# A hybrid diffusion step on one core: attention preparation moved beside the neighbourhood attention, and a changed opening

## The chip, the cores and the metric

One core of one Trainium2 chip runs the whole program in one launch. TensorE is called PE here, VectorE DVE, ScalarE ACT, GpSimd POOL, SyncE SP. The metric is the device time of one execution in microseconds (us); the profile's span is the part of it that the hardware profiler covers.

## The reference: what is computed

Two identical mixer layers (DEPTH = 2, width 2048) over 384 tokens: 128 context tokens and 256 latent tokens. Each layer normalises and modulates x (adaLN), projects it once to 7184 columns, runs four head groups on slices of the projection, gates each, and projects the concatenation back:

```
mod = silu(cond) @ ada_w + ada_b;  shift, scale, gate = split(mod, 3)
xm = rmsnorm(x, norm_w) * (1 + scale) + shift
pr = split_projection(xm @ w_in)
out_a = (rglru(conv(lru_x), forward) + rglru(..., backward)) * silu(lru_gate)
out_b = natten_latent(na_q, na_k, na_v, cache, rpb) * silu(na_gate)      # 4 heads
gq = rmsnorm(gqa_q, qnorm); gk = rmsnorm(gqa_k, knorm)                   # per head
out_c = attention(axial_rope(gq), [axial_rope(gk), cache]) * silu(gqa_gate)
out_d = rmsnorm(mlstm both directions) * sigmoid(ml_o) * silu(ml_gate)
x = x + gate * (concat(out_a, out_b, out_c, out_d) @ w_out)
```

Context tokens use a second conditioning vector and read only context. The caches of keys, values and recurrent states are outputs too. All is fp32.

## The kernel before, in words

PE multiplies fp32 by three rounded products: a weight tile arrives by DMA as `raw`, ACT copies it to a rounded `wh` (L193), POOL subtracts to get the rest `wl` (L1284), and PE adds xh·wh, xl·wh and xh·wl (L1402) into one of four accumulator banks (`acc`) or one of two scratch banks (`s`). The same is done to x: `xh` on ACT, `xl` on DVE (L469).

The modulation matrix is too large to sit on PE's path, so it is streamed as `araw` and summed on DVE, one 128x512 multiply-add at a time, into the PSUM tile `sbp` (L197, the first of a piece at L334). A finished piece is folded by two transposes and two reduces (L347, L348), a small matmul (L302) and a few tiny DVE operations (L305, L308, L312). The first two k-tiles are an exception: PE makes their modulation (`ada_pe`), from which `modulate0` builds the first `xh` and `xl`.

The opening follows a written list, START: "P" steps are pieces of that first modulation, "x" loads, "w" weights, "D" the first DVE modulation pieces, and "r" the multiplication of the x tiles `xr` by the reciprocal root mean square (`unit_rms`, L458): six tiles on DVE in one go, ten tiles later on POOL, in two pieces each, issued from `modulate0` four tiles ahead.

After it, one plan holds weight visits and modulation pieces in order. With each visit the planner's clock moves by PE's estimated time (`tick`), and whenever it has passed a due time the current branch generator is advanced one step: mLSTM, then LRU (`br_lru`), then neighbourhood attention (`br_na`, four heads, each a front of scores on the two `s` banks and a back), then grouped-query attention (`br_gqa`). A step's yield, multiplied by PACE, says how much PE time shall pass to the next. A scheduler then orders each engine's instructions by these positions, and every engine runs its list strictly in that order. Deferred jobs (`defer`) run at a given time of the same clock: `setup_params` (L230), twenty tiny DVE operations that make constants for the LRU and the mLSTM, at 60 us after the start of layer 0's modulation.

`br_gqa` begins with its preparation: 18 ACT squares of 128x128 with an accumulator read each, a square root with a Newton step (L401, L402), 18 DVE multiply-multiplies by root and norm weight, 16 DVE operations of rotary positions (L1034, L1038, L1039). Then come transposes, scores, softmax and the products.

Weights, layer constants and caches travel on SP's queue in issue order; some outputs on ACT's.

## Time and profile before

| what | value |
|---|---|
| three runs | 1468.54, 1468.83, 1475.76 us; median 1468.83 |
| profiled execution | 1480.24 us, span 1478.4 us |
| mean granted PE clock over the span | 0.975 of full |
| PE / DVE / ACT / POOL busy | 96% / 73% / 56% / 62% |

A row of a timeline gives start and duration in us, engine, line, operation, what it writes and reads, and in brackets how long the engine stood idle before it and which engine and tile released it. "xN" means N instructions run together. Lines are those of the kernel before. A granted clock of 1.00 is 2.4 GHz; the other level that the rows show is half of it.

### The profile page before, as it was taken

The page shows a single profiled execution, that of the slowest core. Times are in us where ns is not written, and L with a number is a line of the kernel's source. Part 1 is how long each engine was busy: PE and PEld are TensorE (multiplying, and loading weights), DVE is VectorE, ACT ScalarE, POOL GpSimd, SP SyncE. Part 2 cuts the span into 40 slices and gives each one's busy share as a digit, 9 for nine tenths or more (in the row PEclk, how much of TensorE's full clock was granted, in tenths as well). Part 3 has the DMA queues.
Part 4 walks back from the last instruction along what each step waited for, and adds up shares of the span by engine and source line. Part 5 has one row for each costly group of instructions (what it writes and reads, how often), then busy time and mean ns, then how long its engine had stood idle before and what let it go on. Part 6 is the DMA issues. An engine that isn't in the chain of part 4 may idle for free. (4 is left out here: it accounts for less than half of the span.)

```text
span 1478.4 us, 23865 instructions
## 1 busy us (share of the span) xinstructions
PE 1415.2 (96%) x7999; PEld 1331.2 (90%) x7999; DVE 1080.4 (73%) x2050; ACT 828.1 (56%) x1638; POOL 914.5 (62%) x1242
## 2 busy tenths in 40 slices
PE   6889999899999999999989999999999999899997
PEld 1879999798998799999989999999999789799997
DVE  4889999998899948858568998447667760943533
ACT  4579999765546776553343434234454877363432
POOL 1856666656566765755737666675656774555762
PEclk7899999999999999999999999999999999899999
DMA  8777878686677555565748877654547344355433
GB/s 271 242 231 250 240 230 253 197 253 180 180 209 239 163 165 161 206 222 195 233 130 263 249 243 231 181 159 122 173 142 232 100 128 133 104 175 171 146 122 96
DMA packets 167519, 281.67 MB, mean 191 GB/s; under 512 B 17380, under 2 KB 49380, under 8 KB 167268
## 3 DMA queue, kind: packets, MB, share of 16 engines
q1 hardware_dynamic: 159520, 272.40, 60.4%
...
q8 instruction: 62, 1.02, 0.3%
...
## 5 line engine op out<-in xcount | busy, mean ns | idle before, releaser
L1284 POOL TENSOR_TENSOR wl<-raw,wh 128x256 fp32r<-128x256 f32 (+1 forms) x1152 | 864.9, 785 | 477.5 <-ACT wh L193 414.3
L1402 PE MATMUL acc<-xh,wh 128*128 128x384 f32 x1630 | 568.1, 349 | 20.0 <-ACT xh L193 10.0
L1402 PE MATMUL acc<-xl,wh 128*128 128x384 f32 x1630 | 554.2, 340 | 0.0
L1402 PE MATMUL acc<-xh,wl 128*128 128x384 f32 x1630 | 552.2, 339 | 0.2 <-POOL wl L1284 0.2
L197 DVE SCALAR_TENSOR_TENSOR sbp<-araw,pers,sbp 128x512 f32<-128x512 f32 x690 | 517.6, 750 | 27.2 <-DMA araw<-in_ada_n 15.6
L193 ACT ACTIVATE wh<-raw 128x1024 fp32r<-128x1024 f32 (+2 forms) x304 | 307.0, 1013 | 324.9 <-PE acc L1402 248.6
L1402 PEld LDWEIGHTS acc<-xh,wh 128*128 128x128 f32 x1630 | 309.0, 190 | 25.7 <-ACT xh L193 10.4
L1402 PEld LDWEIGHTS acc<-xl,wh 128*128 128x128 f32 x1630 | 308.6, 189 | 1.5
L1402 PEld LDWEIGHTS acc<-xh,wl 128*128 128x128 f32 x1630 | 308.1, 189 | 1.2 <-POOL wl L1284 1.1
L1402 PE MATMUL acc<-wh,xl 128*128 128x512 f32 (+2 forms) x452 | 165.4, 366 | 5.4 <-DVE xl L469 2.7
L1402 PE MATMUL acc<-wl,xh 128*128 128x512 f32 (+2 forms) x452 | 163.9, 363 | 0.0
L1402 PE MATMUL acc<-wh,xh 128*128 128x512 f32 (+2 forms) x452 | 163.0, 361 | 0.0
L1402 PEld LDWEIGHTS acc<-wh,xl 128*128 128x128 f32 x452 | 88.5, 196 | 19.3 <-DVE xl L469 4.6
L1402 PEld LDWEIGHTS acc<-wl,xh 128*128 128x128 f32 x452 | 88.0, 195 | 12.5
L1402 PEld LDWEIGHTS acc<-wh,xh 128*128 128x128 f32 x452 | 88.0, 195 | 12.1
L197 DVE SCALAR_TENSOR_TENSOR cat<-acc,pers,xold 128x128 f32<-128x128 f32 (+1 forms) x56 | 20.3, 409 | 66.7 <-PE acc L1402 66.7
L193 ACT ACTIVATE cat<-acc 128x384 f32<-128x384 f32 (+1 forms) x94 | 46.2, 495 | 5.4 <-PE acc L1402 4.8
L193 ACT ACT_TABLE_LOAD x26 | 33.4, 1283 | 10.2 <-DVE arena L891 7.9
L193 ACT ACTIVATE xh<-cat 128x384 fp32r<-128x384 f32 x32 | 16.5, 519 | 40.0 <-PE acc L1402 24.0
L389 DVE TENSOR_TENSOR arena<-arena,sq 128x384 f32<-128x384 f32 x38 | 25.8, 679 | 16.0 <-ACT sq L193 14.5
L1402 PE MATMUL s<-xh,wh 128*128 128x384 f32 x98 | 34.1, 348 | 1.2 <-ACT cat L193 1.2
L334 DVE TENSOR_SCALAR sbp<-araw,pers 128x512 f32<-128x512 f32 x46 | 34.3, 745 | 0.2
(338 smaller groups left out, 1824.0 us busy)
## 6 DMA issues: line engine op xcount, KB each, us to landing
...
```

What stands on the lines that cost most here:

```text
L193: return nc.scalar.activation(out, in_, f, bias=bias, scale=scale)
L197: return nc.vector.scalar_tensor_tensor(out, a, s, b, op0=op0, op1=op1)
L334: d = nc.vector.tensor_scalar(acc, raw, sc, None, op0=OP.mult)
L389: eng.tensor_tensor(sqacc, sqacc, s, op=OP.add)
L1284: nc.gpsimd.tensor_tensor(it["lo"][:, kk, cs], raw[:, kk, cs], hv[:, kk, cs], op=OP.subtract)
L1402: last_ev["pe"] = nc.tensor.matmul(out, a, b, start=s0 and i == 0, stop=s1 and i == 2, skip_group_check=not it["first"]).ins
```

## The change

A new generator `gqa_prep` takes the GQA preparation out of `br_gqa` and stands in a side queue of its own (`prepq`), which `tick` advances by its own clock whenever no `br_lru` is among the branch generators; what is left of it is run when `br_gqa` begins. Its steps are smaller. Sums of squares are 9 ACT squares of 128x256 and 9 DVE reduces; the normalisation is 18 ACT copies with a scale and 9 DVE products of 128x256; the rotary part has 24 DVE operations. Its constants `gqk` are loaded at its start, behind the last layer load.

In the opening, `ada_pe` ends with three DVE operations on precomputed `nb0`, DVE normalises four x tiles in step "r" and POOL the other twelve, `setup_params` is deferred to 228 and its DVE operations are ordered behind the last modulation multiply-add issued, PACE is 1.12, and two yields of `br_lru` are longer.

```diff
--- before.py
+++ after.py
@@ -103,8 +103,8 @@
     PRE = {0: True, 1: False}
     KG = {0: [2, 2, 2, 2, 2, 2, 2, 2], 1: [8, 8]}
     START = "PxPPxPPxPPxrPDDwwDD"
-    PACE = 1.1
-    clock = dict(now=0.0, due=0.0)
+    PACE = 1.12
+    clock = dict(now=0.0, due=0.0, side=0.0)
     deferred = []
     backlog = []
 
...
@@ -235,6 +235,11 @@
         nc.vector.tensor_scalar(hbi, P("bi"), 0.5, None, op0=OP.mult)
         nc.vector.tensor_scalar(mln, P("mlnorm"), 0.25, None, op0=OP.mult)
 
+    def late_setup():
+        for ins in traced(setup_params):
+            if ins.engine == mybir.EngineType.DVE:
+                order(ins, last_ev["ada"])
+
 
     ada_acc = dict(done=0)
     last_ev = {}
@@ -256,14 +261,8 @@
                 last_ev["v"] = ins
 
 
-    def ada_final_mod(l, j0, nj):
-        v = mod[:, l, j0:j0 + nj, :]
-        b = P("ada_b", l)[:, j0:j0 + nj]
-        nc.vector.tensor_tensor(v, v, b[:, :, None].to_broadcast([128, nj, 2]), op=OP.add)
-        if 16 <= j0 < 32:
-            nb = P("norm", l)[:, j0 - 16:j0 - 16 + nj]
-            stt(Amul[:, l, j0 - 16:j0 - 16 + nj, :], v, 1.0, nb[:, :, None].to_broadcast([128, nj, 2]),
-                OP.add, OP.mult)
+    nb0 = pers(2)
+    stt(nb0, P("ada_b", 0)[:, 16:18], 1.0, P("norm", 0)[:, 0:2], OP.add, OP.mult)
 
     sbp = pada.tile([128, 1024], F32, name="sbp")
 
@@ -282,9 +281,14 @@
             pt = scr("adat")
             for q in range(4):
                 nc.tensor.transpose(pt[:, 2 * q:2 * q + 2], row[0:2, q * 128:(q + 1) * 128], ident[0:2, 0:2])
-            for i, j0 in enumerate((0, 16)):
-                nc.vector.tensor_copy(mod[:, 0, j0:j0 + 2, :], pt[:, 4 * i:4 * i + 4].rearrange("p (q c) -> p q c", c=2))
-                ada_final_mod(0, j0, 2)
+            pv = pt[:, 0:8].rearrange("p (q c) -> p q c", c=2)
+
+            def per_k(v):
+                return v[:, 0:2][:, :, None].to_broadcast([128, 2, 2])
+
+            nc.vector.tensor_tensor(mod[:, 0, 0:2, :], pv[:, 0:2], per_k(P("ada_b", 0)), op=OP.add)
+            nc.vector.tensor_tensor(Amul[:, 0, 0:2, :], pv[:, 2:4], per_k(P("norm", 0)), op=OP.mult)
+            nc.vector.tensor_tensor(Amul[:, 0, 0:2, :], Amul[:, 0, 0:2, :], per_k(nb0), op=OP.add)
             ada_acc["done"] += 1
 
     quarter = pers(4)
@@ -334,6 +338,7 @@
                 d = nc.vector.tensor_scalar(acc, raw, sc, None, op0=OP.mult)
             else:
                 d = stt(acc, raw, sc, acc, OP.mult, OP.add)
+            last_ev["ada"] = d.ins
             if "v" in last_ev:
                 order(d.ins, last_ev["v"])
 
@@ -467,8 +472,8 @@
                                     op0=OP.mult, op1=OP.add)
         xl[k] = big.tile([128, T], F32R, name=f"xl{k}", tag=f"xl{k}", bufs=1)
         nc.vector.tensor_sub(xl[k], t, xh[k].bitcast(F32))
-        if 6 <= k + 4 < KC:
-            unit_rms(k + 4, nc.gpsimd)
+        if 4 <= k + 2 < KC:
+            unit_rms(k + 2, nc.gpsimd)
 
     def split_cat(k):
         act(xh[k], cat[:, k, :], AF.Copy)
@@ -640,7 +645,7 @@
         lay_seq += [(I["mlk"], 512, "mlk", 1)] + [(I["mlc"][l, h], 258, "mlc", 2) for h in range(4)]
         lay_seq += [(I["lw"][l, g], 512, "lw", 2) for g in range(4)]
         lay_seq += [(I["nac"][l, h, :, 0:576], 576, "nac", 2) for h in range(4)]
-        lay_seq += [(I["gqk"][l], 768, "gqk", 1)] + [(I["gqc"][l, h], 256, "gqc", 2) for h in range(2)]
+        lay_seq += [(I["gqc"][l, h], 256, "gqc", 2) for h in range(2)]
     lay_next = []
     last_dma = {}
 
@@ -870,7 +875,7 @@
                 act(uu[d], aa[d], AF.Tanh, bias=nls4[:, cs], scale=nls4[:, cs])
                 act(aa[d], aa[d], AF.Exp, bias=ls4[:, cs], scale=ls4[:, cs])
                 stt(ww[d], ww[d], 1.0, xc, OP.add, OP.mult)
-                yield 3.0
+                yield 3.0 + 0.5 * d
             if g < 3:
                 xn = conv(g + 1)
             tq = wrk.tile([128, NJ], F32, name="tq", tag="t15", bufs=4)
@@ -898,7 +903,7 @@
             else:
                 nc.vector.tensor_add(cat[:, g, :], hh[0], hh[1])
             mark(g)
-            yield 4.0
+            yield 5.0
         defer(6.0, lambda: nc.scalar.dma_start(O["lru"][l], lout))
 
 
@@ -993,58 +998,71 @@
         yield from attention(front, prep)
 
 
+    def gqa_prep(l):
+        gq, kk = S["gqa_q"], S["gqa_k"]
+        gqk = lay.tile([128, 784], F32, name="gqk", tag="gqk", bufs=1)[:, 0:768]
+        order(nc.sync.dma_start(gqk, I["gqk"][l]).ins, last_dma["d"])
+        nc.scalar.dma_start(O["gqa_v"][l], S["gqa_v"][:, 0, :])
+        ss = slot("gss")
+
+        def pairs(t):
+            for c in range(3):
+                ap = kk[:, t, :] if c == 2 else gq[:, t, c * 256:c * 256 + 256]
+                yield ap, t * 6 + 2 * c, gqk[:, 640:768] if c == 2 else gqk[:, 512:640]
+
+        def tmp(name):
+            return wrk.tile([128, T], F32, name=name, tag="t15", bufs=4)[:, 0:256]
+
+        for t in range(3):
+            for ap, i, _ in pairs(t):
+                sq = tmp("gsq")
+                act(sq, ap, AF.Square)
+                nc.vector.tensor_reduce(ss[:, i:i + 2], sq.rearrange("p (h n) -> p h n", h=2), axis=AX.X, op=OP.add)
+            yield 2.5
+        root = sm(10, 18, "groot")
+        act(root, ss, AF.Sqrt, bias=epsc, scale=1.0 / 128)
+        nc.vector.tensor_scalar(ss, ss, 1.0 / 128, EPS, op0=OP.mult, op1=OP.add)
+        rms_newton(root, ss, sm(11, 18, "gnewt"))
+        rq = root.rearrange("p (t h) -> p t h", t=3)[:, :, 0:4]
+        nc.vector.tensor_scalar(rq, rq, SC, None, op0=OP.mult)
+        yield 3.0
+        for t in range(3):
+            for ap, i, wn in pairs(t):
+                for h in range(2):
+                    hs = slice(h * 128, h * 128 + 128)
+                    act(ap[:, hs], ap[:, hs], AF.Copy, scale=root[:, i + h:i + h + 1])
+                x3 = ap.rearrange("p (h n) -> p h n", h=2)
+                nc.vector.tensor_tensor(x3, x3, wn[:, None, :].to_broadcast([128, 2, 128]), op=OP.mult)
+            yield 3.0
+        for t in range(2):
+            cos = gqk[:, t * 128:(t + 1) * 128]
+            s4 = gqk[:, 256 + t * 128:256 + (t + 1) * 128].rearrange("p (a s f) -> p a s f", a=2, s=2)
+            for ap, _, _ in pairs(1 + t):
+                rot = tmp("rot")
+                r5 = rot.rearrange("p (h a s f) -> p h a s f", h=2, a=2, s=2)
+                x5 = ap.rearrange("p (h a s f) -> p h a s f", h=2, a=2, s=2)
+                for s in range(2):
+                    nc.vector.tensor_tensor(r5[:, :, :, s, :], x5[:, :, :, 1 - s, :],
+                                            s4[:, :, s, :][:, None, :, :].to_broadcast([128, 2, 2, 32]),
+                                            op=OP.mult)
+                x3 = ap.rearrange("p (h n) -> p h n", h=2)
+                nc.vector.tensor_tensor(x3, x3, cos[:, None, :].to_broadcast([128, 2, 128]), op=OP.mult)
+                nc.vector.tensor_add(ap, ap, rot)
+                yield 1.5
+        nc.scalar.dma_start(O["gqa_k"][l], kk[:, 0, :])
+
     def br_gqa(l):
+        while prepq:
+            advance_side()
         gq = S["gqa_q"]
         kk = S["gqa_k"]
         gv = S["gqa_v"]
-        gqk = next_lay()
-        qn, kn = gqk[:, 512:640], gqk[:, 640:768]
-        nc.scalar.dma_start(O["gqa_v"][l], gv[:, 0, :])
-        ss = slot("gss")
-        junk = slot("ktm")
-
...
-        for t in range(2):
-            cos = gqk[:, t * 128:(t + 1) * 128]
-            sin = gqk[:, 256 + t * 128:256 + (t + 1) * 128]
-            for ap, nh, wi in ((gq[:, 1 + t, :], 4, 0), (kk[:, 1 + t, :], 2, 1)):
-                rot = w(wi, "rot")[:, 0:nh * 128]
-                r5 = rot.rearrange("p (h a s f) -> p h a s f", h=nh, a=2, s=2)
-                x5 = ap.rearrange("p (h a s f) -> p h a s f", h=nh, a=2, s=2)
-                s4 = sin.rearrange("p (a s f) -> p a s f", a=2, s=2)
-                for s in range(2):
-                    nc.vector.tensor_tensor(r5[:, :, :, s, :], x5[:, :, :, 1 - s, :],
-                                            s4[:, :, s, :][:, None, :, :].to_broadcast([128, nh, 2, 32]),
-                                            op=OP.mult)
-                x3 = ap.rearrange("p (h n) -> p h n", h=nh)
-                nc.vector.tensor_tensor(x3, x3, cos[:, None, :].to_broadcast([128, nh, 128]), op=OP.mult)
-                nc.vector.tensor_add(ap, ap, rot)
-            yield 4.0
-        nc.scalar.dma_start(O["gqa_k"][l], kk[:, 0, :])
         qT = cm(six("gqT"))
         kT = cm(six("gkT"))
         for h in range(6):
             p_ = scr("gt")
             for t in range(3):
-                ap = heads(t)[h][0]
+                ap = gq[:, t, h * 128:(h + 1) * 128] if h < 4 else kk[:, t, (h - 4) * 128:(h - 3) * 128]
                 nc.tensor.transpose(p_[:, t * 128:(t + 1) * 128], ap, ident)
             act(qT[:, h, :] if h < 4 else kT[:, h - 4, :], p_[:, :T], AF.Copy)
             if h == 5:
@@ -1076,9 +1094,20 @@
 
 
     fillers = []
+    prepq = []
 
     def start(fn):
-        return lambda l: fillers.append(fn(l))
+        def f(l):
+            fillers.append(fn(l))
+            if fn is br_gqa:
+                prepq.append(gqa_prep(l))
+        return f
+
+    def advance_side():
+        try:
+            clock["side"] = max(clock["side"], clock["now"] - 4.0) + PACE * next(prepq[0])
+        except StopIteration:
+            prepq.pop(0)
 
     gk_get = lazy("gqa_k", lambda t: t, lambda key: wts.tile([128, 3, 256], F32, name="gqa_k", tag="gqa_k", bufs=1))
 
@@ -1346,6 +1375,8 @@
             need(*mods[0][1:])
         while fillers and clock["due"] <= clock["now"]:
             advance()
+        while prepq and clock["side"] <= clock["now"] and all(g.__name__ != "br_lru" for g in fillers):
+            advance_side()
 
     accs = {}
     turn = [0, 0]
@@ -1556,7 +1587,7 @@
             upto("w", wl, w_dma, pos["w"] + 1)
         elif tok == "r":
             rstd_bc()
-            for k in range(6):
+            for k in range(4):
                 unit_rms(k, nc.vector)
         elif tok == "P":
             it = first.pop(0)
@@ -1589,7 +1620,7 @@
                 for k in it["ks"]:
                     need(l, k)
                 if l == 0:
-                    defer(60.0, setup_params)
+                    defer(228.0, late_setup)
         elif ty == "split":
             whole.clear()
             for n4 in range(2):
```

DVE in layer 1, kernel before: the end of the fourth neighbourhood-attention head (L986), then the preparation, in which `arena`, `cat` and `gqa_k` are its tiles, and the first gate operation `gth`.

```order
L986 ISA arena,nm<-s_79,nabias 128x384
L986 ISA nm 128x1
L916 RECIPROCAL rs<-ssum 128x3
L1015 TENSOR_SCALAR arena<-arena 128x18
...
L197 SCALAR_TENSOR_TENSOR cat<-cat,arena,gqk 128x128 x4
L197 SCALAR_TENSOR_TENSOR gqa_k<-gqa_k,arena,gqk 128x128 x2
L1034 TENSOR_TENSOR arena<-cat,gqk 128x8x32
...
L1038 TENSOR_TENSOR cat<-cat,gqk 128x512
L197 SCALAR_TENSOR_TENSOR gth<-gth,acc_112 128x384
```

Nothing of the preparation stands among the heads, and the gate waits for its place in the list behind it.

DVE in layer 1, changed kernel: from the second head's scores (L991) over preparation operations to the third head's.

```order
L991 ISA arena,nm<-s_79,nabias 128x384
L991 ISA nm 128x1
L1020 TENSOR_REDUCE arena<-gsq 128x2 x3
...
L1035 TENSOR_TENSOR cat<-cat,gqk 128x256 x2
L1035 TENSOR_TENSOR gqa_k<-gqa_k,gqk 128x256
L1035 TENSOR_TENSOR cat<-cat,gqk 128x256
L1045 TENSOR_TENSOR rot<-cat,gqk 128x4x32 x2
...
L1050 TENSOR_TENSOR cat<-cat,rot 128x256
L988 TENSOR_REDUCE nm<-s_79 128x1
L991 ISA arena,nm<-s_79,nabias 128x384
```

All 42 operations of the preparation now stand between the heads of the neighbourhood attention, and the first gate operation follows the fourth head with no preparation in front:

```order
L1050 TENSOR_TENSOR gqa_k<-gqa_k,rot 128x256
L988 TENSOR_REDUCE nm<-s_80 128x1
L991 ISA arena,nm<-s_80,nabias 128x384
L991 ISA nm 128x1
L991 ISA arena,nm<-s_79,nabias 128x384
L991 ISA nm 128x1
L921 RECIPROCAL rs<-ssum 128x3
L197 SCALAR_TENSOR_TENSOR gth<-gth,acc_113 128x384
```

In these rows `nm` and `s` belong to a head's scores; the gate moved from behind the preparation to behind the head.

DVE in the opening, kernel before: the last two of six x tiles, then the end of `ada_pe` (`pers` holds the modulation), up to the first modulated tile `xmt`.

```order
L458 TENSOR_TENSOR xr_94<-xr_94,pers 128x384
L458 TENSOR_TENSOR xr_95<-xr_95,pers 128x384
L286 COPY pers<-s_80 128x4 x2
L262 TENSOR_TENSOR pers<-pers 128x4
L197 SCALAR_TENSOR_TENSOR sbp<-araw,pers,sbp 128x512
L262 TENSOR_TENSOR pers<-pers 128x4
L197 SCALAR_TENSOR_TENSOR sbp<-araw,pers,sbp 128x512
L197 SCALAR_TENSOR_TENSOR pers<-pers 128x4
L197 SCALAR_TENSOR_TENSOR sbp<-araw,pers,sbp 128x512
L466 TENSOR_SCALAR xmt<-xr_90,pers 128x128
```

The first modulated tile stands behind eight operations here. The same place in the changed kernel, which goes on to the pick that ends the first modulation piece (L309, L305 before):

```order
L463 TENSOR_TENSOR xr_93<-xr_93,pers 128x384
L289 TENSOR_TENSOR pers<-s_80,pers 128x4
L290 TENSOR_TENSOR pers<-s_80,pers 128x4
L291 TENSOR_TENSOR pers<-pers 128x4
L197 SCALAR_TENSOR_TENSOR sbp<-araw,pers,sbp 128x512
L471 TENSOR_SCALAR xmt<-xr_90,pers 128x128
...
L197 SCALAR_TENSOR_TENSOR sbp<-araw,pers,sbp 128x512 x27
...
L338 TENSOR_SCALAR sbp<-araw,pers 128x512 x2
L197 SCALAR_TENSOR_TENSOR sbp<-araw,pers,sbp 128x512 x4
L309 TENSOR_TENSOR picked<-s_80,pers 128x32
```

Three small operations and one `sbp` stand where five and three stood, and the set-up operations, which before were interleaved with `sbp` from here on, are gone. They now stand in layer 0's first mLSTM head (`ls` and `pers` of 128x16):

```order
L717 SCALAR_TENSOR_TENSOR arena<-s_80,pers 128x256
L212 RECIPROCAL ls_3567<-ls_3567 128x16
L721 TENSOR_TENSOR arena<-arena,mlk 128x384
L213 TENSOR_TENSOR ls_3566<-ls_3566,ls_3567 128x16
L721 TENSOR_TENSOR arena<-arena,mlk 128x384
```

L717 and L721 are the scan and product of that head; the set-up stands between them.

## Rows read from the trace of the kernel before

**Rows 1.** Page: busy time of each engine, share of span, instructions.

```profile
PE 1415.2 (96%) x7999; PEld 1331.2 (90%) x7999; DVE 1080.4 (73%) x2050; ACT 828.1 (56%) x1638; POOL 914.5 (62%) x1242
```

**Rows 2.** Timeline, PE: instructions that began after a wait, and one pick.

```profile
39.38 0.69 PE L1402 MATMUL acc<-xh,wh 128*128 128x384 f32 x1 [5.77 <-ACT xh L193]
...
77.58 0.30 PE L302 MATMUL s<-red,pers 128*128 128x32 f32 x2
...
85.61 0.69 PE L1402 MATMUL acc<-xh,wh 128*128 128x384 f32 x1 [4.27 <-ACT xh L193]
...
351.95 0.49 PE L796 MATMUL s<-ml_v,arena 128*128 128x129 f32 x2 [2.28 <-DVE arena L197]
...
496.19 0.69 PE L865 MATMUL s<-xcs,lwh 128*128 128x388 f32 x2 [3.39 <-DVE picked L305]
...
1176.65 1.02 PE L865 MATMUL s<-xcs,lwh 128*128 128x388 f32 x2 [3.13 <-ACT arena L193]
...
1275.78 0.69 PE L1402 MATMUL acc<-xh,wh 128*128 128x384 f32 x1 [6.99 <-DVE gth L197]
```

**Rows 3.** Stretches: us; PE, PEld, DVE, ACT, POOL busy; PE clock; DMA share; GB/s.

```profile
39.38:49.38 10.00, 8.45 (x38) 7.62 (x39) 10.00 (x21) 6.15 (x11) 10.00 (x18) 0.67 0.67 194
85.61:95.61 10.00, 9.35 (x46) 8.54 (x47) 6.18 (x12) 5.75 (x14) 1.26 (x2) 0.76 0.65 231
95.00:260.00 165.00, 165.00 (x963) 159.66 (x962) 153.62 (x259) 156.20 (x323) 108.29 (x151) 1.00 0.79 238
282.48:292.48 10.00, 8.73 (x38) 7.91 (x39) 9.04 (x16) 6.40 (x13) 7.62 (x12) 0.70 0.64 190
351.95:361.95 10.00, 10.00 (x50) 9.88 (x51) 10.00 (x20) 5.19 (x15) 6.59 (x9) 0.83 0.98 298
496.19:506.19 10.00, 10.00 (x39) 8.32 (x40) 9.96 (x19) 7.43 (x12) 6.26 (x8) 0.83 0.44 130
525.00:600.00 75.00, 75.00 (x441) 73.34 (x439) 52.53 (x118) 46.75 (x115) 45.79 (x52) 1.00 0.54 157
1176.65:1186.65 10.00, 10.00 (x33) 8.36 (x34) 2.75 (x5) 8.90 (x16) 5.16 (x7) 0.70 0.46 135
1206.00:1257.00 51.00, 51.00 (x283) 47.07 (x282) 11.41 (x34) 35.89 (x97) 25.69 (x37) 1.00 0.47 135
1275.78:1285.78 10.00, 10.00 (x42) 10.00 (x43) 10.00 (x20) 1.89 (x3) 1.29 (x2) 0.71 0.10 38
```

**Rows 4.** Timeline, DVE, layer 1's preparation.

```profile
1261.30 2.58 DVE L197 SCALAR_TENSOR_TENSOR cat<-cat,arena,gqk 128x128 f32<-128x128 f32 x4
...
1267.37 0.95 DVE L1034 TENSOR_TENSOR arena<-cat,gqk 128x256 f32<-128x256 f32 x1
...
1268.98 0.41 DVE L1034 TENSOR_TENSOR arena<-cat,gqk 128x256 f32<-128x256 f32 x1
...
1275.18 0.54 DVE L197 SCALAR_TENSOR_TENSOR gth<-gth,acc 128x384 f32<-128x384 f32 x1
```

**Rows 5.** Opening: DVE and ACT timeline, and POOL's groups by form (31 to 95).

```profile
31.31 4.43 DVE L458 TENSOR_TENSOR xr<-xr,pers 128x384 f32<-128x384 f32 x6 [0.57 <-ACT pers L193]
...
38.34 1.86 ACT L193 ACTIVATE xh<-xr,pers 128x128 fp32r<-128x128 f32 x4 [1.17 <-DVE pers L197]
...
L458 POOL TENSOR_TENSOR xr<-xr,pers 128x256 f32<-128x256 f32 x10 | 7.4, 737 | 0.0
```

**Rows 6.** Timeline, DVE, end of the first modulation piece.

```profile
76.34 5.51 DVE L197 SCALAR_TENSOR_TENSOR sbp<-araw,pers,sbp 128x512 f32<-128x512 f32 x7
81.75 0.18 DVE L305 TENSOR_TENSOR picked<-s,pers 128x32 f32<-128x32 f32 x1
```

**Rows 7.** Groups of DVE by line, 44 to 68: the set-up's multiply-adds.

```profile
L197 DVE SCALAR_TENSOR_TENSOR ls<-ls,ls 128x16 f32<-128x16 f32 x7 | 3.0, 424 | 0.0
```

**Rows 8.** Timeline, ACT: before the mLSTM wait, and the LRU's table load.

```profile
347.70 1.06 ACT L193 ACTIVATE wh<-raw 128x1024 fp32r<-128x1024 f32 x1 [3.96 <-DMA raw<-in_w_in]
...
1174.72 1.28 ACT L193 ACT_TABLE_LOAD   x1 [2.72 <-DVE arena L891]
```

20 lines of the change are left out of this document (1 added, 19 removed).

## The prediction

> **What bounds the kernel now.** I read the page's busy line first, then the PE instructions that stood idle before they began, then a table of stretches for the clock behind each of those stalls, and last the DVE and ACT lines in front of each stall. The busy line [rows 1] is to show that PE is the bound: busy 1415.2 us of a span of 1478.4, so all its idle time is 1478.4 − 1415.2 = 63.2 us, and nothing that the change does to DVE, ACT or POOL counts unless it lengthens or shortens one of PE's waits. [rows 2] has the six longest waits that the edits can reach: 5.77 us at 39.38 (the first projection matmul), 4.27 at 85.61, 2.28 at 351.95 (mLSTM, layer 0), 3.39 at 496.19 (LRU, layer 0), 3.13 at 1176.65 (LRU, layer 1), 6.99 at 1275.78. They sum to 25.8 us. Behind each, [rows 3] shows PE's granted clock below 1.00 in the ten microseconds that begin with the restart: the lower of the two levels, 1.2 GHz, in place of 2.4. While the clock is halved PE does half as much, so ten microseconds at a mean clock c lose (1 − c)·10: 3.3 (first matmul), 2.4 (85.61), 3.0 (282.48), 1.7 (351.95), 1.7 (496.19), 3.0 (1176.65), 2.9 (1275.78). In stretches in which PE did not stand (95 to 260, 525 to 600, 1206 to 1257) the same column reads 1.00. A removed stall of some us therefore gives back its own length and two or three us more.
>
> **Part by part. K, layer 1's GQA preparation (1257 to 1276).** Up to the fourth neighbourhood-attention (NA) head DVE is nearly free: 11.41 us busy of the 51 from 1206 to 1257 [rows 3]. Then the normalise and rotary operations come in a block, from 128x128 operations at 2.58/4 = 0.65 us each (1261.30) through rotary products, and the gate operation `gth` that frees PE's accumulator bank stands behind them until 1275.18; PE restarts 0.6 us later [rows 2, 4]. In the new order the whole preparation stands ahead of that gate, between the four NA heads' operations. Gone are the 6.99 us and the 2.9 us of low clock: −9.9.
>
> What the moved preparation costs: 9 reduces, 9 norm products and 24 rotary operations on DVE, 42 in all, none longer in elements than 128x256. At 0.41 us (the quicker 128x256 row, 1268.98) they take 42·0.41 = 17.2 us, at 0.95 (the same operation at 1267.37) 42·0.95 = 39.9. DVE's room is 51 − 11.4 = 39.6 us in layer 1 and 75 − 52.5 = 22.5 in layer 0 [rows 3], where part of the old preparation already lies in that stretch. I take the quick end, since POOL works only half of either stretch (25.69 of 51, 45.79 of 75), and book +2 (0 to +5) for NA heads whose scores wait on DVE behind the preparation, in layer 1.
> The same row pair is the place for a rule. 1267.37 and 1268.98 are one operation, with two SBUF inputs, at 0.95 and 0.41 us [rows 4]. The Trainium skill ("SBUF — State Buffer", section "Who interferes with whom") says that a VectorE instruction with two SBUF inputs contends with a GpSimd instruction that reads SBUF, and that whichever starts second is blocked until the other is done. The 0.54 us between the two rows fit that. By the rule every one of the moved products can meet POOL's weight subtraction; what it would do is the slower rival below.
>
> ACT gets 18 scaled copies of 128x128. The nearest row is `xh` at 1.86/4 = 0.47 us each [rows 5]: 8.4 us, and 9 squares of 128x256, between one and two of those each, 4.2 to 8.4. It loses the 18 squares. Two activation-table loads are added as the root falls among the NA exponentials: 1.28 us each by the row at 1174.72 [rows 8]. ACT is free 15.1 us of 51 in layer 1 and 28.2 of 75 in layer 0 [rows 3], so this hides, but not in layer 0 between the last two NA heads: there six norm products and eighteen copies stand in front of the gate evacuations of one PE group. Before, that place cost nothing (PE is busy 75.00 of 75). I book +1.5 (0 to +4). The preparation's own DMA goes on SP's queue behind the last layer load and no longer ahead of the GQA caches; two ACT-queue stores come earlier. Neither has a waiter on PE before the attention: 0.
>
> **A, the opening.** DVE normalises six xr tiles in 4.43 us, 0.74 each, from 31.31, then runs seven small or modulation-weight operations, and ACT's `xh` starts at 38.34 [rows 5]. Four tiles end at 31.31 + 2.95 = 34.26 and three 128x4 operations replace the seven: `xh` can start near 36.5. Gain 1.8 of the 5.77. The low clock behind it stays, since 4 us of idle remain. POOL inherits two tiles, 4 operations at up to 0.74 (its 128x256 mean there) = 3.0 us ahead of weight subtractions that PE needs next; if they land on PE they eat the gain and 1.2 us more, and if low clock goes as well the gain is at most 3. −1.8 (−3 to +2); SP's weight DMAs wait for these subtractions too, and the modulation weights queue behind them.
>
> **B, the stall at 85.61.** PE delivered the sum at 77.58, yet DVE's pick stands behind seven `sbp` operations (5.51 us) until 81.75, a lateness of 4.2 us [rows 2, 6]. DVE was late by the parameter set-up: seven 128x16 operations take 3.0 us, 0.42 each [rows 7]; the other thirteen are no larger, and at half of that or all of it they add 2.8 to 5.5: I take 3, so 6 in all. All twenty leave this stretch, and four `sbp`, not seven, stand before the pick. That covers 4.2 us, so the stall falls to about zero or one, and with it most of the low clock's 2.4: −5.5 (−6.7 to 0; 0 if the modulation-weight transfers, not DVE, set the pace).
> **D, 278 to 292.** The modulation chain ends here; DVE is busy 153.62 of 165 us before it [rows 3]. PE arrives up to 7 us earlier and DVE loses only the set-up and its idle: a small wait may grow. +1 (−2 to +3, the low end if its low clock goes).
> **E, the set-up at its new place.** The twenty operations, 6 us, now stand among mLSTM head 0's DVE chain, ahead of its scores. Before, the 2.28 us at 351.95 came from ACT waiting 3.96 us for a weight transfer [rows 2, 8], so part of the 6 us is covered. +1 (−4 if the wait and its low clock vanish, +4 if all 6 us show but a third).
> **G and J, the LRU steps.** Both stalls are LRU matmuls that wait for banks which the previous head's DVE and ACT operations release late; in J a table load waited 2.72 us for a DVE scan [rows 2, 8]. The longer yields and the slightly larger pace factor put some 2.5 us more of PE's own work into each head's step. G: 3.39 + 1.7 = 5.1 at most, I take −3. J: 3.13 + 3.0 = 6.1 at most, I take −4, since the step's own latency on ACT and DVE stays and only its cover grows.
>
> **Sum** of the profiled run: K −9.9, NA layer 1 +2, layer 0 +1.5, A −1.8, B −5.5, D +1, E +1, G −3, J −4 = −18.7. That execution took 1480.24 us, 11.4 more than the median of the runs shown (1468.83). Its work is the same, so I read the excess as longer waits. Its losses are 63.2 us of idle and about 18 of low clock behind the seven stalls, 81; the median run's would be 70, or 86%. −18.7·0.86 = −16. Forecast 1468.8 − 16 = about 1453 us.
>
> **Rivals.** 1, waits change place: the preparation's 17 us are not hidden but reappear at NA scores and gates, five points of 2 us with low clock after two, while A and B are eaten by DVE's chain (D). For it: DVE's chain is full until 280 and NA's heads take turns on two banks. Against: DVE's 11.41 of 51. New waits 5·2 + 2·1.7 = 13.4 against K's 9.9 and 4 of the LRU's 7: −0.5, about 1468.
> 2, slower: port contention in the NA stages. Mechanism: moved products at 0.95 instead of 0.41 beside POOL's subtractions. Between the second and third head about fifteen large ones stand in a row, 15·0.95 = 14.3 us. A head takes some 13 us of PE's time (51/4), of which DVE has about 10 for this; from there on every head waits. Three waits per layer of 4 us, each with 1.7 of low clock: 2·3·5.7 = 34, against −18.7 − 3.5 that I booked without them: +12 in the profiled run, +10 on the median: 1479. It decides only if over two thirds of the products are blocked; in [rows 4] the quick and slow ones alternate with POOL at half load.
> 3, only K: the opening, B, G and J come back as other waits of the ada chain and the LRU's latency, while the preparation hides: −9.9 + 2 + 1.5, times 0.86, and −3 for what remains: 1460.
> That the change does nothing at all is ruled out by the order: the gate stands behind no preparation any more.
>
> **Chances.** Forecast case 0.58 (1444 to 1461), rival 3 0.16, rival 1 0.15, rival 2 0.11. A measurement of this kernel tells about 0.5%, 7.3 us, from no change, so faster means below 1461.5: nearly all of the forecast case, three quarters of rival 3, a tenth of rival 1: 0.56 + 0.12 + 0.02 = 0.70. Slower is rival 2 with a tenth of rival 1: 0.13. Same: 0.17. Range 1442 to 1471: its low end is the sum with B, E, G and J at their best ends (−29.1·0.86 = −25, so 1444) and a little more, its high end lies just past rival 1 and leaves rival 2 out.
>
> **What would show it.** Right: no PE wait over 2 us between NA's fourth head and the first GQA matmul in layer 1, gate evacuation within 1 us of PE's group end; the pick behind B within a few us of PE's sum; first projection matmul near 37.5; granted clock 1.00 through the LRU of layer 0. Wrong: scores of the third NA head waiting on DVE with the moved products at 0.9 us before them; POOL's subtraction of the third weight as the releaser of an early matmul; mLSTM head 0 waiting over 4 us. The forecast fails upward if two of those hold, downward if D's waits also go.

## The result: slower, and where the time went

The changed kernel took 1481.85 us (median of 6 runs, 1479.82 to 1482.77), the kernel before beside it 1472.3 us (6 runs, 1466.91 to 1477.73): a ratio of 1.0056, 95% interval 1.0028 to 1.0083. Forecast were 1453 us, a range of 1442 to 1471, and a chance of 0.13 for slower. Both the sign and the range were wrong.

One fact of the kernel before is needed to read that number: its own times fall into two groups, near 1467 to 1471 us and near 1474 to 1480 us, and the profile on which the prediction rests (1480.24 us) is of the second group, the median beside it (1468.83) of the first. Where the two groups part is shown with the first experiment; why a run falls into one of them stays open. Against the first group the changed kernel loses 13 us, against the second 5 to 6.

The page's busy line of the changed kernel answers to [rows 1]; PE is still the bound, with 1479.8 − 1414.9 = 64.9 us idle where there were 63.2:

```profile
PE 1414.9 (96%) x7999; PEld 1330.9 (90%) x7999; DVE 1093.5 (74%) x2061; ACT 832.2 (56%) x1620; POOL 916.5 (62%) x1246
```

PE's waits by releaser, changed kernel (columns: instruction, what it waited for, us in total, times, longest):

```profile
PE acc L1433 <- ACT xh L193: 5.6, 2, 2.8
...
PE s L1433 <- POOL wl L1313: 4.6, 2, 3.7
PE s L818 <- ACT arena L193: 4.2, 1, 4.2
PE s L870 <- ACT arena L193: 4.1, 1, 4.1
PE s L937 <- DVE picked L309: 3.1, 1, 3.1
...
PE acc L1433 <- ACT cat L193: 2.5, 1, 2.5
...
PE s L796 <- DVE arena L766: 2.0, 1, 2.0
```

Of [rows 2], 6.99 us at layer 1's gate, 3.13 in layer 1's LRU and 2.28 at 351.95 are gone; the first matmul waits 2.81 us instead of 5.77, and the wait of 4.27 us that ended at 85.61 is now one of 2.79 that ends at 85.89. New are a wait for POOL's `wl` in the opening (3.69), two in mLSTM head 0 (2.01 for DVE, 4.21 for ACT behind POOL's `ss`), one in layer 0's neighbourhood attention (NA, 3.12) and a smaller one in layer 1's (2.46). The LRU wait of layer 0 grew from 3.39 to 4.09. The stretches behind these restarts, as [rows 3] shows them (start:end length, busy us of PE, PEld, DVE, ACT, POOL with counts, PE's granted clock, DMA share, GB/s); the third begins with the wait itself:

```profile
36.43:46.43 10.00, 8.28 (x40) 7.77 (x41) 7.02 (x11) 4.42 (x8) 10.00 (x17) 0.69 0.47 139
51.09:61.09 10.00, 9.95 (x42) 9.44 (x43) 3.49 (x5) 2.68 (x5) 10.00 (x15) 0.74 0.62 178
83.10:93.10 10.00, 6.58 (x32) 6.02 (x33) 9.82 (x20) 4.76 (x13) 2.38 (x4) 0.83 1.00 331
367.89:377.89 10.00, 10.00 (x46) 9.77 (x47) 4.66 (x11) 2.83 (x5) 2.95 (x5) 0.71 0.36 115
516.30:526.30 10.00, 10.00 (x38) 8.27 (x39) 8.76 (x10) 9.91 (x17) 10.00 (x14) 0.83 0.70 188
565.04:575.04 10.00, 10.00 (x51) 9.74 (x52) 7.53 (x16) 5.37 (x13) 5.98 (x8) 0.84 0.46 120
1206.00:1257.00 51.00, 48.54 (x256) 43.58 (x256) 36.36 (x86) 41.73 (x86) 29.71 (x36) 1.00 0.45 128
1257.00:1276.00 19.00, 19.00 (x115) 18.52 (x114) 4.90 (x16) 12.17 (x24) 12.83 (x19) 1.00 0.40 114
```

The stalls at 51.09 and 565.04 each bring a stretch at the lower level where there was none before; the one at 367.89 (0.71 in its row) takes the place of the shorter one behind 351.95 (0.83 in [rows 3]). The two rows of layer 1 stand at 1.00.

To add this up I took, for each stretch of the program, PE's idle time plus half of its busy time while its granted clock was at the lower level. The stretches are cut at the same matmuls in every kernel; worked out so from the profile of each, in us:

| stretch | before (profile shown) | before (first group, e12) | changed | forecast change (before the factor 0.86), from the profile shown | change, from the same |
|---|---|---|---|---|---|
| opening, to the first projection matmul (A) | 21.3 | 20.5 | 18.4 | −1.8 | −2.9 |
| from there to ~100 us (B) | 13.1 | 13.6 | 16.0 | −5.5 | +2.9 |
| end of modulation (D) | 7.0 | 7.1 | 8.6 | +1 | +1.6 |
| mLSTM layer 0 (E) | 5.2 | 4.4 | 11.4 | +1 | +6.2 |
| LRU layer 0 (G) | 5.1 | 3.3 | 6.0 | −3 | +0.9 |
| NA and GQA start, layer 0 | 0.8 | 1.0 | 6.5 | +1.5 | +5.7 |
| LRU layer 1 (J) | 6.5 | 4.8 | 0.0 | −4 | −6.5 |
| NA and GQA start, layer 1 (K) | 9.9 | 0.9 | 2.5 | −7.9 | −7.5 |
| the rest | 20.2 | 18.6 | 18.5 | 0 | −1.7 |
| sum | 89.0 | 74.2 | 87.8 | −18.7 | −1.2 |

Against the first group the sum grows by 13.6 us, which is the measured 13. The remaining PE time (span less the sum) is 1389.3, 1391.0 and 1391.2 in three profiles of before and 1392.0 in the changed kernel's, so some 2 us either way are below what this accounting resolves.

In short: two stalls of layer 1 went (J and K, −14.0 against the profile shown), but 9 us of them are a stall that a run of the first group does not have. New losses of about 6 us each came in the mLSTM and in the NA of layer 0, and the first 100 us gained nothing.

### The profile page after: what moved, and what is told of

The parts are those of the page before. It is cut to its first block, busy times and chain, and to the rows that moved or that the text cites. A ratio compares the mean times of both kernels' runs of the same rounds, so it can differ in the third digit from the quotient of the medians.

```text
span 1479.8 us, 23880 instructions
## 1 busy us (share of the span) xinstructions
PE 1414.9 (96%) x7999; PEld 1330.9 (90%) x7999; DVE 1093.5 (74%) x2061; ACT 832.2 (56%) x1620; POOL 916.5 (62%) x1246
## 4 chain that ended last, share of the span: by engine, by line
PE 59%; DVE 15%; issue 3%; ACT 2%; POOL 2%; DMA 1%; DVEq 0%; SPq 0%; ACTq 0%; POOLq 0%
PE acc L1433 49%; DVE sbp L197 6%; PE acc L1474 2%; POOL wl L1313 2%; PE s L796 1%; PE s L870 1%; PE s L937 1%; ACT wh L193 1%; DVE turned L352 1%; DMA araw<-in_ada_n 1%; DVE red L353 1%; DVE cat L197 1%; DVE xmt L197 1%; DVE arena L197 0%; PE s L951 0%
## 5 line engine op out<-in xcount | busy, mean ns | idle before, releaser
L197 DVE SCALAR_TENSOR_TENSOR sbp<-araw,pers,sbp 128x512 f32<-128x512 f32 x690 | 517.8, 750 | 30.9 <-DMA araw<-in_ada_n 18.7
L1433 PEld LDWEIGHTS acc<-xh,wh 128*128 128x128 f32 x1630 | 308.6, 189 | 18.4 <-ACT xh L193 6.0
L1433 PEld LDWEIGHTS acc<-wh,xh 128*128 128x128 f32 x452 | 87.1, 193 | 11.2
L197 DVE SCALAR_TENSOR_TENSOR cat<-acc,pers,xold 128x128 f32<-128x128 f32 (+1 forms) x56 | 20.2, 409 | 79.6 <-PE acc L1433 79.5
L1433 PE MATMUL s<-xh,wl 128*128 128x384 f32 x98 | 33.7, 347 | 4.6 <-POOL wl L1313 4.6
```

Of the source, the lines that this page charges most:

```text
L197: return nc.vector.scalar_tensor_tensor(out, a, s, b, op0=op0, op1=op1)
L1433: last_ev["pe"] = nc.tensor.matmul(out, a, b, start=s0 and i == 0, stop=s1 and i == 2, skip_group_check=not it["first"]).ins
```

## The experiments

Each ratio is to runs of the kernel before on the same chip. Beside e1 to e4 these are mostly of the second group (median 1476.36), beside e5 to e8 and e9 to e12 nearly all of the first (1468.70 and 1468.93). The letters in the expectations name theories: M is mostly the one held likelier, the others are its rivals.

**e1 and e12: the kernel before, unchanged, on two chips.**

> The kernel before, unchanged, once more. Theory M (misplaced waits): the two layer-1 stalls that the change removed (3.13 us at the LRU, 6.99 us behind the fourth attention head, with 3.0 and 2.9 us of low clock behind them) belong to the order of the instructions, so they come back within 1 us of those lengths, and the time is 1467 to 1478 us. Rival V (variation): those stalls were long only in the one profiled execution, which took 1480.2 us against a median of 1472.3; then in this profile one of the two is shorter by at least 4 us.

> The kernel before, unchanged, a third time. Theory T (two tempos in one place): its runs are of two kinds, 1467 to 1470 and 1474 to 1479 us, and they differ behind the fourth attention head of layer 1: where DVE's products with two SBUF inputs run at 0.65 and 0.95 us beside POOL's subtractions at 0.8, PE waits 7 us; where they run at 0.28 and 0.42 and POOL's take 1.4, PE waits under 2. If this profile is of a run under 1471, it shows the second, if of one over 1474, the first. Rival W: both kinds wait 7 us there and differ elsewhere.

e1: 1476.17 us (12 runs, 1474.67 to 1479.60), 1.0008 [0.9994, 1.0021]; its profile has both layer-1 stalls, 3.12 and 6.98 us. e12: 1469.26 us (11 runs, 1467.20 to 1470.14), 0.9999 [0.9990, 1.0008]; its profile waits 0.90 us at the gate. Beside the kernels on e1's chip stood 29 further runs of before, median 1476.36, of which six lie between 1467.6 and 1470.1 and the others above 1474; on e12's chip 15 of 16 lie below 1471.1 and one at 1476.2, and on the third chip (e5 to e8) 28 of 29 and one at 1476.64. Both groups come up on each of the three, but how often differs much from chip to chip. So the gate's stall belongs to a run and not to the kernel, as theory T had it; the evidence is three profiles of the kernel before, one by one, and e7's below, which differs in the opening alone and also waits only 0.88 us there. Where they part stands in DVE's rows of e12, with the same operations in the same order as [rows 4] (start, us, engine, line, operation):

```profile
1256.96 1.14 DVE L197 SCALAR_TENSOR_TENSOR cat<-cat,arena,gqk 128x128 f32<-128x128 f32 x4
...
1260.12 0.42 DVE L1034 TENSOR_TENSOR arena<-cat,gqk 128x256 f32<-128x256 f32 x1
...
1264.75 0.55 DVE L197 SCALAR_TENSOR_TENSOR gth<-gth,acc 128x384 f32<-128x384 f32 x1
```

Four norm products take 1.14 us here and 2.58 in [rows 4]; from them to `gth` it is 7.8 us here and 13.9 there. POOL's groups over the same work (count, busy us, mean ns, idle before) show the other side, first e12 (1255 to 1272), then the profile shown before (1257 to 1274):

```profile
L1284 POOL TENSOR_TENSOR wl<-raw,wh 128x256 fp32r<-128x256 f32 x9 | 15.2, 1722 | 2.5 <-ACT wh L193 2.5
```

```profile
L1284 POOL TENSOR_TENSOR wl<-raw,wh 128x256 fp32r<-128x256 f32 x15 | 12.3, 846 | 4.5 <-ACT wh L193 3.4 <-PE acc L1402 1.1
```

In e12 POOL's subtractions take 1.72 us each and DVE's products run free; in the other run DVE's are stretched and POOL's take 0.85. By the rule that the prediction takes from the Trainium skill ("SBUF — State Buffer", section "Who interferes with whom"), of two such instructions the one that starts second is blocked; the traces agree in that one engine's operations are stretched and the other's are not, and add that over a whole block of operations it can be either engine's. They do not show the order of the starts, and 1.72 us is more than a subtraction that runs alone (0.70, the four at 50.28 below) and one product of 0.28 together.

**e2: six tiles on DVE in the opening, as before (changed kernel otherwise).**

```
-        if 4 <= k + 2 < KC:   unit_rms(k + 2, nc.gpsimd)
+        if 6 <= k + 4 < KC:   unit_rms(k + 4, nc.gpsimd)
...
-            for k in range(4):    # unit_rms on DVE
+            for k in range(6):
```

> The changed kernel with six x tiles normalised on DVE and ten on POOL, as before. Theory M: the wait of 3.69 us for POOL's third weight and the 2 us of low clock behind it go, the first projection matmul moves back by 1.5 us (36.4 to 37.9), so 4 us are gained by 57 us; of them 2 to 4 are left at the end, 1478 to 1480 against 1481.9. Rival C (the modulation chain sets the pace up to 280 us): the wait at 83 us grows by what was gained, PE stands at the same time at 100 us and the end stays at 1481 to 1483.

1480.33 us (1476.74 to 1483.14), 1.0040 [1.0022, 1.0059]. The wait for `wl` at 47 us went, but the first matmul moved from 36.4 back to 39.07 and the stall that begins at 83 grew from 2.79 to 4.19. Opening and what follows it, up to 100 us, lose 35.2 us in e2, 34.4 in the changed kernel, 34.4 before, and in the profiles of all runs of this document it is between 33.0 and 35.5: the edits move the loss about within the first 100 us and take nothing from it, as theory C expected. (The time itself, 1480.33, lies between what the two theories gave.) DVE's modulation-weight multiply-adds show how (groups, 40 to 86 us: count, busy us, mean ns, idle before and its releaser), in before, the changed kernel and e2:

```profile
L197 DVE SCALAR_TENSOR_TENSOR sbp<-araw,pers,sbp 128x512 f32<-128x512 f32 x39 | 29.2, 750 | 4.6 <-DMA araw<-in_ada_n 4.1
```

```profile
L197 DVE SCALAR_TENSOR_TENSOR sbp<-araw,pers,sbp 128x512 f32<-128x512 f32 x37 | 27.9, 754 | 13.0 <-DMA araw<-in_ada_n 11.9
```

```profile
L197 DVE SCALAR_TENSOR_TENSOR sbp<-araw,pers,sbp 128x512 f32<-128x512 f32 x39 | 29.4, 755 | 8.8 <-DMA araw<-in_ada_n 7.7
```

With the set-up gone DVE waits for the weights' transfers 7.8 us longer (11.9 against 4.1), and 3.6 longer in e2, where two more tiles fill the time: the set-up had stood where DVE would have waited. So the pick that the prediction wanted earlier comes at 81.49 in the changed kernel and at 81.75 before [rows 6]:

```profile
81.49 0.18 DVE L309 TENSOR_TENSOR picked<-s,pers 128x32 f32<-128x32 f32 x1
```

What holds these transfers up stands in SP's queue. It issues in order, and between the modulation weights stand the projection's, whose buffers come free only when POOL has subtracted. The queue's waits for that between 30 and 95 us (columns as in PE's list above), before and changed:

```profile
SPq L1271 <- POOL wl L1284: 17.8, 8, 6.0
```

```profile
SPq L1300 <- POOL wl L1313: 30.5, 11, 8.6
```

The changed kernel's longest, 8.6 us, ends with the issue at 53.12, just when POOL's third `wl` is done; DVE then waits for the weights issued right behind it:

```profile
53.12 0.38 SPq L1300 DMA_DIRECT2D raw<-in_w_in  x1
53.59 0.42 SPq L1322 DMA_DIRECT2D araw<-in_ada_n  x1
```

```profile
57.70 1.54 DVE L197 SCALAR_TENSOR_TENSOR sbp<-araw,pers,sbp 128x512 f32<-128x512 f32 x2 [4.56 <-DMA araw<-in_ada_n]
```

So POOL, busy 10.00 of 10 us behind 36.43 and again behind 51.09, is late for DVE's stream too, by way of SP. This is read from the traces; no run took tiles off POOL, and e2, with ten tiles on it as before, still has 25.7 us of these waits.

That the first matmul's new early start is paid back by POOL directly as well is in the changed kernel's timelines of POOL and PE:

```profile
42.51 7.84 POOL L463 TENSOR_TENSOR xr<-xr,pers 128x256 f32<-128x256 f32 x14
50.28 2.81 POOL L1313 TENSOR_TENSOR wl<-raw,wh 128x256 fp32r<-128x256 f32 x4
```

```profile
51.09 0.69 PE L1433 MATMUL s<-xh,wl 128*128 128x384 f32 x1 [3.69 <-POOL wl L1313]
```

Fourteen pieces of the tiles (128x128 and 128x256, shown under one shape) stand in a block ahead of the third weight's `wl`; before there were eight, in 4.26 us.

**e3: the parameter set-up early (changed kernel otherwise).**

```
-                    defer(228.0, late_setup)
+                    defer(60.0, setup_params)
```

> The changed kernel with the parameter set-up at 60 again, where it stood before. Theory M: the set-up's 6 us in the first mLSTM head cost 6.2 us (idle and low clock from 300 to 425 us: 11.4 against 5.2 before); with it early again this stretch falls back to 5 to 7 us, the wait near 83 us grows by 1 to 3 us, in all 1477 to 1479 against 1481.9. Rival L: the first mLSTM head is late because of the weight transfers, as it was before; then the stretch stays at 10 us or more and the time within 2 us of 1482.

1479.00 us (1473.55 to 1488.87), 1.0030 [1.0006, 1.0053]; a wide spread. Its profile, of the quickest of these runs (span 1471.8), tells more than its time: the mLSTM stretch falls from 11.4 to 5.2 us, its waits of 2.01 and 4.21 are gone, and up to 100 us it loses 34.5 (stall from 82.72, 4.21), as every other version. So the late set-up costs 6 us in mLSTM and saves nothing in the opening. How it costs them, changed kernel, DVE, POOL, ACT and PE:

```profile
346.34 0.72 DVE L219 TENSOR_SCALAR ls<-pers 128x16 f32<-128x16 f32 x1
...
348.63 0.70 DVE L232 TENSOR_SCALAR pers<-pers 128x16 f32<-128x16 f32 x1
```

```profile
344.03 8.69 POOL L1313 TENSOR_TENSOR wl<-raw,wh 128x256 fp32r<-128x256 f32 x12 [4.97 <-ACT wh L193]
```

```profile
350.98 0.71 PE L796 MATMUL s<-mlc,arena 128*128 128x129 f32 x4 [2.01 <-DVE arena L766]
...
367.43 0.98 ACT L193 ACTIVATE arena<-arena,ss 128x128 f32<-128x128 f32 x3 [4.18 <-POOL ss L810]
367.89 0.47 PE L818 MATMUL s<-pers,arena 128*128 128x128 f32 x1 [4.21 <-ACT arena L193]
```

The set-up's 20 operations take 6.2 us on DVE between 337.07 and 350.01, from 0.15 us when POOL is quiet to 0.73 beside its subtractions. The estimate of 6 us was right; that most of it would be covered was wrong, since the head's scores and then its normalisation run one after the other. The last scores (L767) are done at 351.12, where they were done at 342.58 before, and PE had not that much to spare. At the second wait DVE has `ss` ready at 364.01, but POOL takes it up only at 366.55, behind subtractions and a product of the LRU.

**e4 and e10: the new preparation kept for layer 1 alone.** e4 runs layer 0's in the new form at the GQA's start; e10 has the old form there, as the kernel before.

```
# e4, in br_gqa (e10 has the old lines of the preparation there)
+        if l == 0:
+            yield from gqa_prep(l)
...
# e4 and e10, where the side queue is filled
-            if fn is br_gqa:
+            if fn is br_gqa and l == 1:
                 prepq.append(gqa_prep(l))
```

> The changed kernel with the GQA preparation of layer 0 run at the start of the grouped-query attention instead of beside the neighbourhood attention; layer 1 as changed. Theory M: in layer 0 nothing was waiting for the preparation (0.8 us lost between 525 and 710 before, 6.5 in the changed kernel), so 4 to 6 us come back: 1476 to 1478 against 1481.9. Rival N: the lost time there comes from the late load of the neighbourhood constants and from the longer LRU steps, not from the preparation; then 561.9's wait of 3.1 us stays and the time is within 2 us of 1482.

> The changed kernel with layer 0's preparation written and placed as before (its squares, norm and rotary in the old form at the start of the grouped-query attention, its constants loaded in the old place); layer 1 as changed. Theory M: the 6.5 us lost in layer 0's attention fall to about 1, so 5 us come back: 1476 to 1478 against 1481.9. Rival N: the longer LRU steps and the set-up cause that loss; then 4 us or more of it stay and the time is 1480 or more.

e4: 1484.66 us (1482.82 to 1486.30), 1.0065 [1.0041, 1.0089]. e10: 1482.89 us (1482.63 to 1484.12), 1.0098 [1.0082, 1.0113]. The wait of 3.12 us goes in both. In e4 waits of 2.19 us (from 611.87, for a rotary sum of DVE) and 1.35 come in its place, and NA and GQA start lose 6.4 us where they lost 6.5; in e10 it is one of 4.78 us at the GQA's first products, and 8.2 us. Both expectations that these runs would gain 4 to 6 us failed; rival N of e10 came true. Layer 0's loss is therefore not the moved preparation's alone: with the old preparation in its old place it is larger, though the kernel before loses 0.8 there. The wait that the moved preparation makes, changed kernel, DVE and PE:

```profile
561.75 0.56 DVE L973 TENSOR_TENSOR nabias<-nac 128x384 f32<-128x384 f32 x1 [2.72 <-DMA nac<-in_nac]
...
564.46 0.42 DVE L1035 TENSOR_TENSOR gqa_k<-gqa_k,gqk 128x256 f32<-128x256 f32 x1 [1.75 <-ACT gqa_k L193]
564.80 0.18 DVE L309 TENSOR_TENSOR picked<-s,pers 128x32 f32<-128x32 f32 x1
...
565.04 1.12 PE L937 MATMUL s<-pers,arena 128*128 128x128 f32 x4 [3.12 <-DVE picked L309]
```

DVE runs in order: the modulation's pick, which holds PE's scratch bank, stands behind a preparation product that waits for ACT's scaled copy, and behind a bias that waits for its transfer.

**e5: yields and pace factor as before, new preparation kept (changed kernel otherwise).**

```
-    PACE = 1.12
+    PACE = 1.1
...
-                yield 3.0 + 0.5 * d
+                yield 3.0
...
-            yield 5.0
+            yield 4.0
```

> The changed kernel with the LRU's yields and the pace factor as before (3.0, 4.0, 1.1). Theory Y: the longer yields alone removed the LRU's stall in layer 1 (6.5 us lost from 1140 to 1206 before, 0.0 in the changed kernel), so 5 to 7 us of it come back there; in layer 0 the same stretch changes by less than 2 us; in all 1485 to 1488 against 1481.9. Rival P: the stall went because the preparation's squares left ACT's list; then it stays gone and the time is 1480 to 1483.

1495.42 us (1493.08 to 1495.94), 1.0173 [1.0153, 1.0193]: the slowest of all, and 7 us above the 1485 to 1488 expected. Layer 1's LRU loses 4.8 us again, which shows J; but layer 0's LRU and NA lose 9.4 and 11.1 (6.0 and 6.5 in the changed kernel). The waits of e5:

```profile
PE s L870 <- ACT arena L193: 7.8, 4, 3.1
PE s L818 <- ACT arena L193: 7.1, 5, 4.2
...
PE s L306 <- ACT arena L193: 4.1, 1, 4.1
```

So the changed layer 0 does worse with the short steps than with the long ones. The set-up is late here as well, and the preparation does not run while the LRU does, so which of them makes the LRU slower than before is not shown.

**e11: three parts undone.** The changed kernel with e10's old layer-0 preparation, the set-up in its old place and e2's six tiles; three-operation modulation, yields, pace factor and layer 1's preparation stay.

```
-            if fn is br_gqa:
+            if fn is br_gqa and l == 1:   # layer 0: the old preparation in br_gqa
...
-            for k in range(4):
+            for k in range(6):
...
-                    defer(228.0, late_setup)
+                    defer(60.0, setup_params)
```

> The changed kernel without its three costs as I see them: layer 0's preparation as before, set-up at 60, six x tiles on DVE; what is left is the three-operation modulation, layer 1's preparation, the longer yields in both layers. Theory M: 5 us from the attention, 6 from the mLSTM, 1 to 2 from the opening: 1467 to 1471 against 1481.9, no better than the kernel before where that does not stall in layer 1. Rival R: the longer yields in layer 0 cost by themselves; then the LRU and attention stretches of layer 0 keep more than 8 us of loss and the time stays over 1473.

1476.01 us (1474.39 to 1476.67), 1.0050 [1.0037, 1.0062]: still slower than before, by 7 us. mLSTM is back at 4.1 (from 12.8 in e10, which differs by set-up and tiles alone), layer 1's LRU at 0.0, but NA and GQA start of layer 0 lose 7.9 against 0.8 to 1.0 before. What is left of the change costs nothing there in the runs that have it alone (e6 0.7, e7 1.3), except the longer yields with the larger pace factor: by elimination these cost it, as rival R had it. No run has the two alone, none tells between them, and the parts do not add up: with the new preparation in layer 0, e5 loses more without them. PE and DVE of e11 there:

```profile
607.46 0.69 PE L1109 MATMUL s<-pers,cat 128*128 128x128 f32 x2 [4.81 <-DVE cat L1100]
```

```profile
598.22 2.58 DVE L197 SCALAR_TENSOR_TENSOR cat<-cat,arena,gqk 128x128 f32<-128x128 f32 x4
```

The same norm products, groups of 560 to 660 us, first of the kernel before, then of e11:

```profile
L197 DVE SCALAR_TENSOR_TENSOR cat<-cat,arena,gqk 128x128 f32<-128x128 f32 x12 | 4.3, 418 | 0.0
```

```profile
L197 DVE SCALAR_TENSOR_TENSOR cat<-cat,arena,gqk 128x128 f32<-128x128 f32 x12 | 5.8, 542 | 0.0
```

With nothing of layer 0's preparation changed, its products are stretched more: 418 ns become 542, which is 1.5 us of the 4.8 us wait. The larger part is that the preparation starts later against PE's progress. Its first DVE operation, before and in e11:

```profile
582.88 0.16 DVE L1015 TENSOR_SCALAR arena<-arena 128x18 f32<-128x18 f32 x1
```

```profile
594.08 0.28 DVE L1076 TENSOR_SCALAR arena<-arena 128x18 f32<-128x18 f32 x1 [0.30 <-ACT arena L193]
```

It is 11.2 us later, while PE comes to the first matmuls that need the result only 2.6 us later, at 602.65 (607.46 − 4.81) in place of 600.06. That longer steps put the end of NA, and with it this start, later is the likely cause; it was not tried apart.

**e6, e7, e8: parts of the change alone, on the kernel before.** e6 moves layer 1's preparation beside its NA (layer 0 stays as it was); e7 has only the three-operation modulation; e8 is e6 with the longer yields in layer 1 alone:

```
# e8, beside e6's edit
-                yield 3.0
+                yield 3.0 + 0.5 * d * l
...
-            yield 4.0
+            yield 4.0 + l
```

> The kernel before with one edit alone: layer 1's GQA preparation runs beside the neighbourhood attention; layer 0, opening, set-up, yields as before. Theory M: the 9.9 us lost between 1206 and 1300 shrink to 2 to 4 us, all else stays, so 6 to 8 us are gained: 1468 to 1470 against 1476.4. Rival S (waits only change place): without the longer LRU steps the preparation runs into the next wait, less than 2 us are gained: 1475 to 1477.

> The kernel before with one edit alone: the first modulation ends in three DVE operations in place of five. Theory C (the modulation weights' transfers set the pace of the first 95 us): the first projection matmul comes about 1 us earlier (39.4 to 38.4), the wait near 81 us grows by as much, the losses up to 100 us stay at 34 to 35 us and the time at 1475 to 1477. Rival O: the microsecond is kept, the losses up to 100 us fall to 33 and the time to 1474 to 1475.5.

> The kernel before with two edits, both in layer 1 only: the preparation beside the neighbourhood attention and the longer LRU yields. Theory M: both layer-1 stalls go (6.5 and 7 us), and nothing new is paid in layer 0 and the opening, so 11 to 14 us are gained: 1462 to 1466 against 1476.4. Rival S: the stretches after them take back half, 1469 to 1471.

e6: 1467.37 us (1464.86 to 1471.77), 0.9989 [0.9976, 1.0002] beside runs of before of the first group. NA and the GQA's start in layer 1 lose 0.00 us. Windows of e6 (columns as above):

```profile
1206.00:1257.00 51.00, 51.00 (x291) 47.78 (x290) 24.29 (x72) 40.90 (x94) 28.26 (x36) 1.00 0.42 126
1257.00:1276.00 19.00, 19.00 (x118) 18.72 (x117) 11.15 (x22) 12.34 (x29) 10.48 (x14) 1.00 0.58 199
```

PE is busy 70 of 70 us: the preparation hides in layer 1 at no cost. e6 has the lowest median of all versions, and against before's first group its gain is within what can be told from none; none of its 12 runs was above 1471.8, so the second group did not show.
e7: 1470.53 us (1468.32 to 1473.61), 1.0009 [0.9998, 1.0020]: the shorter modulation does nothing that can be told from none.
e8: 1469.14 us (1467.32 to 1470.48), 1.0000 [0.9989, 1.0011]. Layer 1's LRU loses 0.6 us instead of 4.8, and NA 5.2 instead of none. ACT and PE of e8:

```profile
1226.13 1.28 ACT L193 ACT_TABLE_LOAD   x1
...
1231.71 0.47 ACT L193 ACTIVATE cat<-s 128x384 f32<-128x384 f32 x1
```

```profile
1232.23 0.79 PE L980 MATMUL s<-nac,na_q 128*128 128x128 f32 x2 [2.62 <-ACT cat L193]
```

The copy `cat<-s` that brings NA's result out of the bank stands behind the root's table load and the scaled copies. Longer steps change which NA head the root falls into, and this time it falls badly.

**e9: the changed kernel again.**

> The changed kernel, unchanged, once more, beside the three others here. Theory M: its losses lie where they lay: 11 us from the start of the mLSTM to its end, 6 in the LRU and 6 to 7 in the attention of layer 0; time 1480 to 1483. Rival V: one of these three is shorter by 4 us or more.

1482.34 us (1481.42 to 1482.60), 1.0094 [1.0080, 1.0107]. The ratio is larger than the first one because nearly all runs of before beside it were of the first group; its own time is the same, and its losses agree with the table (mLSTM 12.9, NA layer 0 6.3, layer 1 2.4, LRU layer 1 0).

## Why the prediction was wrong, by its steps

- **Base of the sum: wrong, and worth 9 us.** The step "its work is the same, so I read the excess as longer waits" and the factor 0.86 spread the profile's excess of 11.4 us over all stalls. The larger part was at one place: K's stall is 9.9 us in that run and 0.9 in a run like those of the median (e12), 9.0 of the 14.8 us by which the two sums of the table differ. Half of the forecast gain did not exist in the runs that it was subtracted from.
- **K, mechanism and size right in layer 1 for the run that the sum was made from.** −7.5 against −7.9 with the +2 for NA, which came as one wait of 2.46 us. For a run of the first group there were 0.9 us to gain, and the changed kernel loses 1.6 more there. No wait over 1 us stands between 1257 and the GQA's first matmul. The moved two-input products took 0.28 us (128x128) and 0.41 to 0.78 us (128x256, means of groups) in layer 1, between the two ends, half of the groups at the quick one that I chose. Rival 2 (contention in every NA head) did not decide.
- **J right in sign, short by 2.5.** e5 shows it by undoing it, e8 by doing it alone (0.6 us in place of 4.8).
- **G failed.** Booked was −3. The same yields that clear layer 1's LRU give +0.9 in layer 0's (+2.7 against the first group), and, with the pace factor and the old preparation, cost some 7 us in the NA and GQA behind it (e11, by elimination). I costed the yields only at the LRU's own waits and not at what stands beside later operations when the LRU ends later.
- **NA of layer 0: +1.5 booked (0 to +4), +5.7 measured.** The place was named (gate evacuations behind the copies on ACT), and what it missed is DVE's queue: products that wait for ACT hold up the pick behind them, as the rows at 564 show. That is 3.12 us and the low clock behind it; without the move the yields make a loss as large in the same stretch.
- **E failed: +1 booked (−4 to +4), +6.2 measured**, by e3 and e10 against e11. The 6 us of work were right, the cover was not: the wait of 3.96 us on ACT lay behind the head's scores, and the set-up stands in front of them, so it covered nothing of the scores' delay.
- **B failed in its cause.** The step said "DVE was late by the parameter set-up". The changed kernel and e2 show that it would have waited for the modulation weights' transfers instead: 7.8 us more once the set-up is gone, and 3.6 more in e2. The prediction had named that case as the upper end (0) and chose the other one; it came out beyond that end, at +2.9, as POOL's pieces stand before `wl`. Under A it had also written that SP's weight transfers wait for POOL's subtractions and the modulation weights queue behind them; it gave that no price, and the queue's waits for POOL grew from 17.8 to 30.5 us.
- **A right alone (−2.9), and paid back within B.** Together they come to 0.0 where −7.3 stood. POOL's inherited 3 us were sized well (the block ahead of `wl` grew from 4.26 to 7.84), but booked as free, and the case in which they land on PE was left to the range. The watched sign for it, POOL's subtraction of the third weight as a releaser, is there: 3.69 us.
- **Rival 1 was nearest**, waits that change place, with A and B eaten. But it put the new waits in NA alone and the opening's loss on DVE's chain; they came in mLSTM, in layer 0's NA, and in the opening behind POOL.
